# A fused QKV projection on one Trainium2 core: the K index renumbered, and the weights loaded one k-slice per transfer

## The chip, the cores and the metric

The kernel runs on one core of one Trainium2 chip, with one launch. The core has TensorE (PE, with its weight loads shown apart as PEld), VectorE (DVE), ScalarE (ACT), GpSimd (POOL) and SyncE (SP, which here only issues transfers), and sixteen DMA engines that move data between HBM and the on-chip SBUF. The metric is the device time of one execution in microseconds (us); lower is better.

## The reference

```python
batch, seq, hidden = 16, 512, 768
x: (16, 512, 768) float32,   w_qkv: (768, 2304) float32

qkv = np.matmul(x, w_qkv)
q = qkv[..., :hidden]; k = qkv[..., hidden:2*hidden]; v = qkv[..., 2*hidden:]
return np.stack([q, k, v], axis=0)          # (3, 16, 512, 768) float32
```

It is one product of 8192 rows by K = 768 by 2304 columns, whose three thirds of columns go to three places.

## The kernel before

**Tiling.** The 8192 rows of x are taken 256 at a time: 32 pairs of row tiles, p = 0 to 31. K = 768 is cut into KT = 6 slices of 128. The columns are cut into two "quads" of 1024 (q = 0 and 1, each two blocks of CB = 512, c = 0 and 1) and REM = 256 columns between them. PE contracts over the partition axis, so both operands must have k on the partitions. Which k lies on which partition is free, as long as x and w agree: before, partition p, slice j holds k = 6p + j.

**The weights.** `load_w` (L87) issues one transfer on SP for a range of slices of one column block. `load_blocks` (L93) calls it: for (q, c) = (0, 0) with one slice per transfer (six transfers of 256 KB), for the other three blocks with three slices per transfer (two of 768 KB each). The 256 remaining columns, tile `str`, come in one transfer with six slices. All of w is 7.08 MB, loaded once in the first part of the program. fp32 staging tiles `st` are then cast: into `b1` and `bt` (bf16, by DVE at L413 and L373, by ACT at L371), `b22` (L441, L456), `w_rem` (L426, L427), and differences t1 to t4 for the second method (`sum_w`, L113).

**The first three pairs (p = 0, 1, 2)** run plainly in bf16, in `block` (L375): the six row tiles times one 512-column block at a time, in the order (q, c) = (0,0), (0,1), (1,0), (1,1). Their x comes by `load_rows` (L138) with rows on the partitions; `cast_rows` (L153) makes bf16 (DVE L145 and L149, ACT L147), `turn_rows` (L160) has PE transpose 128x128 tiles (L167) and copies them out of PSUM. Eleven and then four matmuls on zeros (`busy`, L361) stand before real work.

**All later pairs (p = 3 to 31)** use Strassen's seven products with Winograd's sums (`do`, L220; matmuls L212), two in bf16 and five in fp32r, for both quads at once (`two`, L275), and `rem` (L260 to L273) for the other 256 columns. Their x comes by `load_x` (L122): four transfers per pair, each putting a quarter of the columns, 192, on 32 partitions. Then `transpose` (L128, instruction L130) turns 32x32 blocks on DVE, `round_x` (L173, instruction L175) casts to bf16 on POOL, and `sums_x` (L177) forms the sums on POOL.

**What sets the order.** The order is written out by hand; each engine and each issuing queue takes its instructions in the program's order. On SP: `load_rows(0)`, `load_rows(1)`, six transfers of block (0,0), `str`, `load_rows(2)`, then blocks (0,1), (1,0), (1,1), `load_x(3)`, the stores of remaining columns and of block results, with `load_x(4)` among them. On ACT, `block` puts the casts of the next block (`cast_next`, L409) ahead of the evictions of the even row tiles (L394) of p = 0 and 1. The pool `o` has five buffers; `str` and six quads of the first three pairs share them, so the fifth and sixth quads wait for stored ones. `bt0` and `bt1` share one buffer. PSUM has eight banks.

Of the kernel before, what the change touches and what calls it, by code (L numbers as in the profile page):

```python
# [10 lines left out]
def kernel(  # L11
# [20 lines left out]
    nc = tc.nc  # L32
    P = 128
    G = 32
    B, T, H = x.shape
    M = B * T
    K = H
    N3 = w_qkv.shape[1]
    KT = K // P
# [45 lines left out]


    def load_w(dst, j0, nj, off, cols):  # L87
        rows = w_qkv.rearrange("(p j) n -> p j n", j=KT)
        nc.sync.dma_start(dst, rows[:, j0:j0 + nj, off:off + cols])

    stage = {}

    def load_blocks(q, c, nj=KH):  # L93
        if q == 0:
            t = tq_pool.tile([P, KT, CB], fp32, name="st0", tag="tq")
            for j in range(0, KT, nj):
                load_w(t[:, j:j + nj], j, nj, Q_OFF[q] + c * CB, CB)
            stage[q, 0, c], stage[q, 1, c] = t[:, :KH, :], t[:, KH:, :]
        else:
            for h in range(2):  # L100
                t = st_pool.tile([P, KH, CB], fp32, name="st1", tag="st")
                load_w(t[:], h * KH, KH, Q_OFF[q] + c * CB, CB)
                stage[q, h, c] = t[:]
# [11 lines left out]
    xin, xf, xb, sr = {}, {}, {}, {}  # L115
# [12 lines left out]
    def transpose(p):  # L128
        t = xf_pool.tile([P, KT, 2 * P], fp32, name="xf")
        nc.vector.transpose(  # L130
            t[:].rearrange("p j (g b) -> p g j b", b=G),
            xin.pop(p)[:].rearrange("p g (a j) -> p g j a", a=G),
        )
        xf[p] = t

# [7 lines left out]
    def copy_halves(dst, src, two):  # L143

        nc.vector.tensor_copy(out=dst[0], in_=src[0])  # L145
        if two:
            nc.scalar.activation(dst[1], src[1], ident)  # L147
        else:
            nc.vector.tensor_copy(out=dst[1], in_=src[1])  # L149

    xc = {}

    def cast_rows(p, two=True):  # L153
        src = xin.pop(p)
        xc[p] = s_pool.tile([P, 2, K], bf16, name="xc", tag="s")
        for r in range(2):
            halves = (slice(0, K // 2), slice(K // 2, K))
            copy_halves([xc[p][:, r, n] for n in halves], [src[:, r, n] for n in halves], two)

    def turn_rows(p, two=True):  # L160
        c = xc.pop(p)
        xb[p] = xb_pool.tile([P, KT, 2 * P], bf16, name="xb", tag="xb")
        for r in range(2):
            cols = c[:, r, :].rearrange("m (p j) -> m j p", j=KT)
            ps = ps_pool.tile([P, KT, P], bf16, name="ps")
            for j in range(KT):
                nc.tensor.transpose(ps[:, j, :], cols[:, j, :], eye)  # L167
            ks = (slice(0, KH), slice(KH, KT))
            copy_halves(
                [xb[p][:, n, r * P:(r + 1) * P] for n in ks], [ps[:, n, :] for n in ks], two  # L170
            )
# [179 lines left out]
    load_blocks(0, 0, 1)  # L351
    st_rem = o_pool.tile([P, KT, REM], fp32, name="str", tag="o")
    load_w(st_rem[:], 0, KT, R_OFF, REM)
    load_rows(2)
    load_blocks(0, 1)
# [59 lines left out]
    nothing = lambda p: None  # L415
    busy(11)
    cast_rows(0)
    turn_rows(0)
    busy(4)
    cast_rows(1)  # L420
    cast_k(0)
    cast_k(1)
    turn_rows(1)
    for j in range(2, KT):
        cast_k(j)
# [6 lines left out]
    rem(0)  # L432
    rem(1)
    cast_rows(2, False)
    turn_rows(2, False)
    block(0, 0, b1[0], halves((4, 5)), nothing)
    for h in range(2):
# [11 lines left out]
    sum_w(1, 1)  # L449
    sum_w(1, 2)  # L450
    transpose(3)
    round_x(3)
    sums_x(3)
# [4 lines left out]
    for p in range(NS, NP):  # L458
        def early():
            if p + 1 < NP:  # L460
                transpose(p + 1)
                round_x(p + 1)
                sums_x(p + 1)
            if p + 2 < NP:
                load_x(p + 2, nc.scalar)

        if p < NP - 1:
            two(quad(p, 0), quad(p, 1), early)
        else:
            last(quad(p, 0), quad(p, 1))  # L470
# [30 lines left out]
```

## Time and profile before

| what | value |
|---|---|
| three timed runs | 362.67, 362.73, 363.09 us; median 362.73 |
| the profiled execution: span, first to last instruction | 361.3 us |
| around the span, against that median | 1.4 us |
| PE busy | 353.4 us, 98% of the span |
| DVE, ACT, POOL busy | 224.4, 182.9, 173.9 us |
| `STREAM_TRANSPOSE` L130 on DVE | 29 times, 2950 ns each |
| HBM read, written | 32.24 MB, 75.50 MB |

The profile's own total time is not listed apart from the three timed runs, so its span is set against their median. Busy time is the time in which an engine had an instruction in work. The chain that ended last is followed backwards from the final instruction to whatever released it; shares of that chain say where the time is set, while busy shares of engines off the chain say only how much room they have. A time at which a transfer lands is read from the first instruction that waited for it.

### The profile page before, as it was taken

The numbers are of one execution on the slowest core, as the hardware profiler recorded it, in microseconds if no ns is written. First come the engines' busy times: TensorE is split into PE (matmuls) and PEld (weight loads), VectorE is DVE, ScalarE is ACT, GpSimd is POOL, SyncE is SP. The second block draws the span as 40 slices with busy tenths as digits, with TensorE's granted clock in tenths as the row PEclk, the third lists the DMA queues.
The fourth block names the chain that finished last, engine by engine and source line by source line (L and its number), as shares of the span: only waits on it lengthen the run. The fifth ranks groups of instructions, "written<-read, shape, count | busy, mean of one in ns | idle before, by whom it ended". The sixth has DMA issues, their size and how long they took to land.

```text
span 361.3 us, 5221 instructions
## 1 busy us (share of the span) xinstructions
PE 353.4 (98%) x1765; PEld 251.0 (69%) x1797; DVE 224.4 (62%) x239; ACT 182.9 (51%) x304; POOL 173.9 (48%) x180
## 2 busy tenths in 40 slices
PE   8999999999999999999999999999999999999995
PEld 3644577777777777777777777777777777777763
DVE  3499826765566765566675565676556676556642
ACT  4547555455454545454545445455545454545452
POOL 0001861746664445664445665444665444666410
PEclk9999999999999999999999999999999999999999
DMA  7999869988898999899899999998989899999666
GB/s 298 405 388 373 286 221 359 331 289 295 278 328 301 294 273 294 276 324 315 280 280 290 281 308 309 291 289 278 292 288 321 295 300 271 297 272 339 264 261 232
DMA packets 80617, 108.08 MB, mean 299 GB/s; under 512 B 4816, under 2 KB 60368, under 8 KB 80592
## 3 DMA queue, kind: packets, MB, share of 16 engines
q1 hardware_dynamic: 65184, 96.35, 80.8%
q10 hardware_dynamic: 15408, 11.41, 9.6%
q8 instruction: 14, 0.23, 0.3%
q14 instruction: 11, 0.09, 0.1%
HBM read 32.24 MB, written 75.50 MB: 298 GB/s over the span
## 4 chain that ended last, share of the span: by engine, by line
PE 96%; ACT 1%; issue 1%; ACTq 0%; DVE 0%
PE ps L212 75%; PE ps L262 11%; PE ps L385 9%; PE ps L365 1%; PE ps L167 1%; ACT o L243 0%; ACTq L303 0%; ACT xb L147 0%; ACT orem L317 0%; DVE xb L145 0%; ACT xc L147 0%; ACTq L319 0%; DVE zero L346 0%; ACTq L317 0%
## 5 line engine op out<-in xcount | busy, mean ns | idle before, releaser
L212 PE MATMUL ps<-t,s 128*128 128x512 f32 x696 | 173.8, 398 | 0.0
L212 PEld LDWEIGHTS ps<-t,s 128*128 128x128 f32 x696 | 130.7, 188 | 29.7
L175 POOL CAST xb<-xf 128x1536 bf16<-128x1536 f32 x29 | 43.8, 1510 | 168.3 <-DVE xf L130 156.0
L240 DVE TENSOR_TENSOR o<-o,ps 128x512 f32<-128x512 f32 x58 | 39.9, 688 | 91.2 <-ACT o L239 91.2
L130 DVE STREAM_TRANSPOSE xf<-xin 128x1536 f32<-128x1536 f32 x29 | 85.5, 2950 | 3.7 <-DMA out_dram<-orem 2.1
L212 PE MATMUL ps<-b,xb 128*128 128x512 bf16 x320 | 82.4, 380 | 1.5
L239 ACT ACTIVATE o<-ps 128x512 f32<-128x512 f32 x58 | 34.8, 600 | 44.2 <-PE ps L212 44.2
L212 PEld LDWEIGHTS <-xb 128*128 128x128 bf16 x348 | 31.7, 98 | 35.6 <-issue 7.3
L233 ACT ACTIVATE o<-ps 128x512 f32<-128x512 f32 x58 | 34.9, 601 | 42.1 <-PE ps L212 39.4
L246 DVE TENSOR_TENSOR o<-o,ps 128x512 f32<-128x512 f32 x58 | 39.9, 688 | 21.3 <-PE ps L212 20.2
L212 PE MATMUL ps<-b,s 128*128 128x512 f32 x174 | 48.7, 389 | 0.0
L262 PE MATMUL ps<-w_rem,xb 128*128 128x256 bf16 x384 | 47.2, 273 | 0.0
L243 ACT ACTIVATE o<-ps 128x512 f32<-128x512 f32 x58 | 34.7, 599 | 24.1 <-PE ps L212 21.3
L226 ACT ACTIVATE o<-ps 128x512 f32<-128x512 f32 x58 | 34.7, 598 | 23.8 <-DVE o L246 20.6
L262 PEld LDWEIGHTS <-xb 128*128 128x128 bf16 x384 | 37.4, 98 | 11.2 <-issue 0.5
L230 DVE TENSOR_TENSOR o<-o,ps 128x512 f32<-128x512 f32 x58 | 36.5, 673 | 5.4 <-PE ps L212 4.1
L212 PEld LDWEIGHTS ps<-b,s 128*128 128x128 f32 x174 | 32.7, 188 | 6.8
L184 POOL TENSOR_TENSOR s<-s,xf 128x384 fp32r<-128x384 f32 x29 | 30.0, 1035 | 2.3
L183 POOL TENSOR_TENSOR s<-xf 128x384 fp32r<-128x384 f32 x29 | 30.9, 1064 | 0.0
L185 POOL TENSOR_TENSOR s<-xf 128x384 fp32r<-128x384 f32 x29 | 29.5, 1017 | 0.0
L187 POOL TENSOR_TENSOR s<-xf,s 128x384 fp32r<-128x384 f32 x29 | 29.5, 1016 | 0.0
L272 ACT ACTIVATE orem<-ps 128x512 f32<-128x512 f32 x31 | 18.5, 598 | 20.7 <-PE ps L262 19.5
(36 smaller groups left out, 129.4 us busy)
## 6 DMA issues: line engine op xcount, KB each, us to landing
out_dram<-o SPq DMA_DIRECT2D x62, 768.0 KB, 4.8
out_dram<-o SPq DMA_DIRECT2D x65, 256.0 KB, 4.1
xin<-in_x_dram SPq DMA_DIRECT2D x62, 192.0 KB, 6.9
xin<-in_x_dram ACTq DMA_DIRECT2D x54, 192.0 KB, 4.4
out_dram<-orem SPq DMA_DIRECT2D x31, 256.0 KB, 5.7
st<-in_w_qkv_dram SPq DMA_DIRECT2D x6, 768.0 KB, 13.1
xin<-in_x_dram SPq DMA_DIRECT2D x3, 768.0 KB, 5.7
st<-in_w_qkv_dram SPq DMA_DIRECT2D x6, 256.0 KB, 6.1
```

Of the source, the lines that this page charges most:

```text
L130: nc.vector.transpose(t[:].rearrange("p j (g b) -> p g j b", b=G), xin.pop(p)[:].rearrange("p g (a j) -> p g j a", a=G),)
L175: nc.gpsimd.tensor_copy(out=xb[p][:], in_=xf[p][:])
L212: nc.tensor.matmul(ps[:], lhs[j], rhs[j], start=(start and j == 0), stop=(j == KH - 1), skip_group_check=True,)
L226: nc.scalar.activation(c11, u.x[:], ident)
L230: nc.vector.tensor_tensor(c11, c11, u.z[:], op=add)
L233: nc.scalar.activation(c12, u.x[:], ident)
L239: nc.scalar.activation(c22, u.x[:], ident)
L240: nc.vector.tensor_tensor(c22, c22, u.y[:], op=add)
L243: nc.scalar.activation(c21, u.x[:], ident)
L246: nc.vector.tensor_tensor(c12, c12, u.y[:], op=add)
L262: nc.tensor.matmul(ps, xb[p][:, j, r * P:(r + 1) * P], w_rem[j // KH][:, j % KH, :], start=(j == 0), stop=(j == KT - 1), skip_group_check= ...
L385: nc.tensor.matmul(ps[n][:], xb[p][:, j, r * P:(r + 1) * P], w[:, j, :], start=(j == 0), stop=(j == KT - 1), skip_group_check=True,)
```

## The change

The K index is numbered anew: k = 192 i + 32 j + a, with i in 0..3, j in 0..5, a in 0..31. Partition 32 i + a, slice j holds that k. So:

- `load_w` sees w as four bands of 192 rows; slice j takes 32 neighbouring rows from each band. It issues one transfer per slice where it issued one for a range of slices: `str` becomes six transfers of 128 KB, and the blocks (0,1), (1,0) and (1,1) become six of 256 KB each where they were two of 768 KB. Block (0,0) had six transfers and keeps six, with the new rows.
- `transpose` reads, for each 32x32 block, 32 neighbouring fp32 elements of a partition where it read every sixth one.
- `cast_rows` writes its bf16 columns in the order (j, i, a), while it reads them in the order of k; each half is two of the four bands.
- `turn_rows` then takes 128 neighbouring columns for slice j where it took every sixth one.

```diff
     def load_w(dst, j0, nj, off, cols):
-        rows = w_qkv.rearrange("(p j) n -> p j n", j=KT)
-        nc.sync.dma_start(dst, rows[:, j0:j0 + nj, off:off + cols])
+        rows = w_qkv.rearrange("(i j a) n -> i a j n", i=4, a=G)
+        for j in range(nj):
+            nc.sync.dma_start(dst[:, j], rows[:, :, j0 + j, off:off + cols])
...
         nc.vector.transpose(
             t[:].rearrange("p j (g b) -> p g j b", b=G),
-            xin.pop(p)[:].rearrange("p g (a j) -> p g j a", a=G),
+            xin.pop(p)[:].rearrange("p g (j a) -> p g j a", a=G),
         )
...
         for r in range(2):
-            halves = (slice(0, K // 2), slice(K // 2, K))
-            copy_halves([xc[p][:, r, n] for n in halves], [src[:, r, n] for n in halves], two)
+            turned = xc[p][:, r].rearrange("m (j i a) -> m i j a", i=4, a=G)
+            rows = src[:, r].rearrange("m (i j a) -> m i j a", i=4, a=G)
+            halves = (slice(0, 2), slice(2, 4))
+            copy_halves([turned[:, n] for n in halves], [rows[:, n] for n in halves], two)
...
-            cols = c[:, r, :].rearrange("m (p j) -> m j p", j=KT)
+            cols = c[:, r, :].rearrange("m (j p) -> m j p", j=KT)
```

## The prediction

> **What bounds the kernel now.** I read the page's chain first, to see which engine sets the end; then the chain in order of time, to see whether any stretch differs; then the timeline where the first three pairs end; then the busy time by stretches of the start, where all of w is loaded.
>
> The page, parts 1 and 4 (shares of the span), and three rows of part 6 (issues, KB each, median us to landing):
>
> ```profile
> PE 353.4 (98%) x1765; PEld 251.0 (69%) x1797; DVE 224.4 (62%) x239; ACT 182.9 (51%) x304; POOL 173.9 (48%) x180
> ...
> PE 96%; ACT 1%; issue 1%; ACTq 0%; DVE 0%
> ...
> st<-in_w_qkv_dram SPq DMA_DIRECT2D x6, 768.0 KB, 13.1
> xin<-in_x_dram SPq DMA_DIRECT2D x3, 768.0 KB, 5.7
> st<-in_w_qkv_dram SPq DMA_DIRECT2D x6, 256.0 KB, 6.1
> ```
>
> PE sets 96% of the chain, so DVE's 224 us count for nothing unless something late on DVE reaches PE. In order of time the chain runs through PE without a gap of more than 0.1 us from 18.5 us to the end of the last pair. The timeline (start, us, engine, line) at the end of the first three pairs:
>
> ```profile
> 28.42 7.93 PE L385 MATMUL ps<-b,xb 128*128 128x512 bf16 x35
> ...
> 34.29 1.48 ACT L371 ACTIVATE bt<-st 128x1536 bf16<-128x1536 f32 x1
> ...
> 36.19 7.93 PE L385 MATMUL ps<-bt,xb 128*128 128x512 bf16 x35
> ...
> 43.96 1.47 PE L262 MATMUL ps<-w_rem,xb 128*128 128x256 bf16 x12
> ...
> 45.27 1.46 PE L212 MATMUL ps<-b,xb 128*128 128x512 bf16 x6
> ```
>
> The reader sees two things: the last piece of w that PE needs is cast at 34.29, by ACT, which waited for no transfer there (the page of waits has 0.4 us for `st` in all); and Strassen pair p = 3 begins at 45.4. From there each pair takes 10.74 us of PE. Last, the start by stretches (busy us of each engine, granted clock, DMA share, GB/s):
>
> ```profile
> 2.40:5.00 2.60, 2.60 (x7) 0.91 (x6) 0.09 (x1) 0.09 (x1) 0.00 (x0) 1.00 0.97 376
> ...
> 10.00:15.00 5.00, 4.95 (x26) 2.48 (x26) 2.00 (x6) 2.20 (x4) 0.00 (x0) 1.00 1.06 403
> 15.00:20.00 5.00, 4.83 (x41) 3.46 (x41) 3.38 (x10) 2.19 (x5) 0.00 (x0) 1.00 1.05 406
> 20.00:25.00 5.00, 5.00 (x25) 2.29 (x24) 4.97 (x4) 2.68 (x3) 0.00 (x0) 1.00 1.05 406
> ...
> 240.00:280.00 40.00, 39.79 (x201) 29.82 (x203) 24.87 (x26) 20.16 (x35) 22.89 (x24) 1.00 0.93 300
> ```
>
> From 2.4 us the sixteen DMA engines are full at 403 to 406 GB/s until w is in: 25.3 GB/s for each engine. The start is thus a race of the loads against PE, and PE wins it by little.
>
> **The change part by part.**
>
> *The DVE transposes.* 29 of 2950 ns. The nearest row that reads neighbouring fp32 elements of the same size, the 128x1536 differences of L113, takes 1751 ns; at that, 29 x 1.2 = 35 us of DVE work go. Bounds: 0 and 35 us off DVE. On the time I put nothing, since PE waits for no transpose after p = 3; POOL waits 156 us in all for L130, but POOL itself has 187 us to spare. If DVE's room were gone, the cost would be the wait of L175. PE's 10.74 us per pair remain.
>
> *The casts of the first rows.* Four DVE and four ACT casts for p = 0, 1 (354 and 516 ns) and four on DVE for p = 2. Written in runs of 32 they may slow on DVE. From 384 to 1536 elements a DVE cast goes from 354 to 953 ns, 0.52 ns an element and 154 ns of start; L113's row gives (1751 - 154)/1536 = 1.04 ns an element. At that rate a cast takes 553 ns, so four lose 0.8 us: bounds 0 and 0.8. PE's reads of `xc` gain neighbouring columns: weight loads L167 take 132 ns against 98 ns on `xb`, 24 on the chain, 0 to 0.8 us saved. I take zero for both: what follows hides them, since PE will wait for w.
>
> *Loading w.* This is the step that decides. The number of packets, their size (2 KB, 1 KB for `str`) and the bytes stay. What moves is the number of issues on SP, 13 to 30, and the shape. An issue costs SP 0.4 to 0.5 us where the ring is not full, so 17 more are about 8 us of SP; by bytes the w transfers alone keep SP waiting, so this is hidden if the transfers still run at full width. But the shape changes: until now both sides of every transfer begin with a count that sixteen divides (128 or 768 rows of w, 32 or 128 of x). Now the HBM side begins with four bands whose distance, 192 rows, cannot be folded with the 32 rows inside; the SBUF side begins with 128. No row of before shows how such a transfer is dealt out. The ends are sixteen engines (405 GB/s, nothing lost) and one engine for each band, four (4 x 25.3 = 101 GB/s). I take four: the only cut that falls on the leading step of both sides is that into the four bands, and every full-width row has a leading count that sixteen divides, so none speaks for sixteen here.
>
> [...]
>
> *What four engines make of the start.* Each of those four carries, in SP's order, in KB of 1024: x rows 0 and 1, 96; block (0,0), 6 x 64 = 384; `str`, 6 x 32 = 192; x rows 2, 48; then 384 for each of (0,1), (1,0), (1,1). Together 1872 KB = 1.917 MB, at 25.3 GB/s 75.8 us. Data begins at 2.4; the first x rows (0.786 MB at 405 GB/s, done by 4.3) were used at 4.92, so 0.6 us from bytes to use. The last half block is usable at 2.4 + 75.8 + 0.6 = 78.8 us.
>
> Its cast on ACT (L371) started at 34.29 and now starts at 78.8: 44.5 us later. Against that, PE has run ahead with the first half of block (1,1), whose data come 7.8 us earlier. It gets as far as four of the six row tiles, because the evictions that free further banks stand behind that cast on ACT: 12 matmuls of 0.216 us, 2.6 us gained. For some 5 us before that cast PE has nothing to do. The first eleven matmuls of the trace, after idleness, took 4.88 us, against 11 x 0.216 = 2.38: 2.5 us lost to a slow start. The bounds are 0 and 2.5; I take 2.0, near the only start that the trace has, less a little because the first six wait for banks anyway. (The stretches print a granted clock of 1.00 there too, so the column will not show it.)
>
> [...]
>
> Queued behind the loads on SP are `load_x(3)`, two stores of remaining columns, three quads' stores (64 KB per engine each, 2.6 us), `load_x(4)`. On the four late engines `load_x(3)` lands near 81; then L130, L175 (2.8 us the first time) bring xb to 84 to 86, against p = 3's start at 89. The first quad's store lands near 85, and the eviction of the sixth quad waits for its buffer: 0 to 3 us, inside the same wait, so nothing added, 3 kept for the upper end. From p = 3 on nothing differs, and there the DMA engines, at 0.93 share, take the backlog of stores within a pair or two.
>
> Sum: 44.5 - 2.6 + 2.0 = 43.9 us. Span 361.3 + 43.9 = 405.2; with the 1.4 us between this span and the median of the runs, 406.6.
>
> **The rivals.**
>
> *Sixteen engines, and a gain (faster).* Place: PE's transposes of the first rows, which stand on the chain. Price: up to 0.8 us, 361.9. It decides only if the transfers keep full width, and if PE then finds the first slices of b1 in place (cast at 7.96, first used at 9.3: 0.5 us to spare). Against it: the leading count of four.
>
> *Sixteen engines, nothing to see.* The gain is eaten by slower casts, and `str` in six issues (6 x 0.45 for 0.65 us) pushes `load_rows(2)` by up to 1 us, about the slack that its casts have (done at 16.0, PE free at 17.0). 362.7, within 0.2%; a little more push gives 363.5. For it: packets are unchanged and SP is held back by full rings anyway.
>
> *Eight engines.* 144 + 6912/8 = 1008 KB per engine, 40.8 us, usable at 43.8: 9.5 us late, 372 us. I see no cut into eight in either pattern.
>
> *Four engines at another rate* is a bound, not a rival: if an engine alone is faster than its sixteenth (shares over 1.00 say that packets overlap; I allow 7%), 5 us less, and without the slow start 2 less: 399. Slower: the steady stretch moves 300 GB/s at 0.93, 20.2 GB/s per engine, which would give 425; but it holds 768-byte packets, w does not, so I go half way: 416, with the buffer wait 418.
>
> **How the numbers follow.** Four engines 0.86; eight 0.03; sixteen with a loss over 0.2% 0.03, unchanged 0.06, gain 0.02. So slower 0.92, same 0.06, faster 0.02, where 0.2% (0.7 us) is about what a measurement can tell from no change. Range 398 to 418, holding most of the first case, some 0.82; prediction 406.6.
>
> **What would show it.** In the profile after: DMA at about a quarter of its share and near 100 GB/s from some 6 to 75 us; ACT's and DVE's casts of `st` waiting for transfers of w; PE busy in under half of that stretch; L371's last cast near 79; p = 3 near 89; L130 shorter, near 1.75 us, with DVE's total down by some 35 us and pairs still 10.74 us apart. Wrong if DMA runs at 400 GB/s through 25 us: then the bands do not narrow the transfer, and the time stays within 1 us of before.

## The result, and the profile after

The changed kernel takes 410.28 us (median of four runs, 410.12 to 411.08) against 362.70 us before (362.50 to 363.09): 1.132 times as long, 95% interval 1.130 to 1.133. The profiled execution took 410.42 us, with a span of 408.6. (One of the ten executions of the second experiment below ran at a lower granted clock, 0.85, took 406.21 us and is left out of its median.)

The page of the changed kernel, busy time (part 1), PE's busy tenths, granted clock, DMA share and GB/s in 40 slices of 10.2 us (part 2), the chain by engine and line (part 4), and the issues of the staging tiles (part 6, without a time to landing here). Lines of the code stand three further down than before: L90 issues w, L131 is the DVE transpose, L374 ACT's casts of w, L388 the matmuls of the first three pairs, L215 those of the later ones.

```profile
PE 369.1 (90%) x1765; PEld 254.5 (62%) x1797; DVE 194.9 (48%) x239; ACT 182.0 (45%) x304; POOL 173.6 (42%) x180
...
PE   7548576579999999999999999999999999999995
...
PEclk9856966969999999999999999999999999999999
DMA  5252222798999889999998999999999899999956
GB/s 192 102 148 104 102 102 102 222 340 276 366 374 323 294 292 292 294 286 289 287 291 298 293 293 286 288 288 305 308 297 305 290 296 290 293 296 297 309 211 255
...
PE 77%; SPq 15%; DMA 4%; issue 1%; ACT 1%; ACTq 0%
PE ps L215 66%; SPq L90 15%; PE ps L265 9%; DMA st<-in_w_qkv_dram 4%; PE ps L388 2%; SPq L142 1%; ACT o L246 0%; ACTq L306 0%; ACT orem L320 0%; ACT o L397 0%; ACTq L322 0%; ACTq L320 0%; ACT bt L374 0%
...
st<-in_w_qkv_dram SPq DMA_DIRECT2D x24, 256.0 KB
```

Nearly a fifth of the chain, which was PE from end to end, now belongs to w: SP stands in L90, where an issue takes 2.44 us in the median (ns, min/median/max, in the view of the tile `st`), about the 2.57 us in which 256 KB move at 102 GB/s, and then the last transfer lands:

```profile
L90 SPq DMA_DIRECT2D st<-in_w_qkv_dram x24: 537/2442/4392, 1.7 to 65.5; - x24
```

The damage lies in the first nine slices; from the tenth on PE reads 9 in every slice but the last, as before. The same in stretches (busy us by engine, granted clock, DMA share, GB/s):

```profile
2.40:5.00 2.60, 2.60 (x7) 0.91 (x6) 0.01 (x1) 0.01 (x1) 0.00 (x0) 1.00 0.95 373
...
10.00:20.00 10.00, 5.27 (x15) 1.86 (x16) 1.96 (x7) 0.87 (x2) 0.00 (x0) 0.83 0.26 102
...
40.00:50.00 10.00, 4.96 (x23) 1.97 (x21) 2.17 (x3) 1.19 (x2) 0.00 (x0) 1.00 0.26 102
...
80.00:90.00 10.00, 6.16 (x18) 2.44 (x19) 7.87 (x4) 4.71 (x8) 4.17 (x2) 0.66 1.00 370
...
240.00:280.00 40.00, 39.79 (x200) 29.18 (x203) 22.78 (x28) 19.75 (x34) 20.49 (x21) 1.00 0.93 292
```

The first row is x, at full width (share 0.95, 373 GB/s). Then w flows at 102 GB/s, and the DMA share of 0.26 says how much of the engines that takes: as much as four of sixteen, each as busy as before (1.05 x 4/16 = 0.26). The share is a mean over the engines, and no view lists them one by one; that few of them work, and not all of them a little, is the author's reading, and the probe of the leading count below fits it. (A packet of 2 KB took 84 ns in the median in both traces.) The timeline at the end of the first three pairs (start, us, engine, line):

```profile
64.16 1.48 ACT L374 ACTIVATE b<-st 128x1536 bf16<-128x1536 f32 x1 [5.25 <-DMA st<-in_w_qkv_dram]
...
71.85 1.48 ACT L374 ACTIVATE bt<-st 128x1536 bf16<-128x1536 f32 x1 [4.26 <-DMA st<-in_w_qkv_dram]
...
73.92 2.75 PE L388 MATMUL ps<-bt,xb 128*128 128x512 bf16 x12
...
81.60 1.48 ACT L374 ACTIVATE bt<-st 128x1536 bf16<-128x1536 f32 x1 [7.29 <-DMA st<-in_w_qkv_dram]
...
91.17 1.47 PE L265 MATMUL ps<-w_rem,xb 128*128 128x256 bf16 x12
92.48 1.46 PE L215 MATMUL ps<-b,xb 128*128 128x512 bf16 x6
```

The last cast of w starts at 81.60 (34.29 before), after 7.29 us of waiting for its transfer, and p = 3 begins at 92.65 by the chain (45.43 before). The two pieces of the chains, first the kernel before, then the changed one:

```profile
45.43 1.30 PE ps L212 x6
```

```profile
92.65 1.29 PE ps L215 x6
```

From there to the end of the span it is 315.95 us, before 315.87: nothing in the steady part has changed, although DVE's 29 transposes fell from 2950 to 1772 ns each.

### The profile page after: what moved, and what is told of

It reads as the page before. It is cut to its first block, busy times and chain, and to the rows that moved or that the text cites. A ratio compares the mean times of both kernels' runs of the same rounds, so it can differ in the third digit from the quotient of the medians.

```text
span 408.6 us, 5248 instructions
## 1 busy us (share of the span) xinstructions
PE 369.1 (90%) x1765; PEld 254.5 (62%) x1797; DVE 194.9 (48%) x239; ACT 182.0 (45%) x304; POOL 173.6 (42%) x180
## 4 chain that ended last, share of the span: by engine, by line
PE 77%; SPq 15%; DMA 4%; issue 1%; ACT 1%; ACTq 0%
PE ps L215 66%; SPq L90 15%; PE ps L265 9%; DMA st<-in_w_qkv_dram 4%; PE ps L388 2%; SPq L142 1%; ACT o L246 0%; ACTq L306 0%; ACT orem L320 0%; ACT o L397 0%; ACTq L322 0%; ACTq L320 0%; ACT bt L374 0%
## 5 line engine op out<-in xcount | busy, mean ns | idle before, releaser
L215 PE MATMUL ps<-t,s 128*128 128x512 f32 x696 | 173.8, 398 | 0.0
L215 PEld LDWEIGHTS ps<-t,s 128*128 128x128 f32 x696 | 130.8, 188 | 29.7
L215 PE MATMUL ps<-b,xb 128*128 128x512 bf16 x320 | 82.6, 380 | 1.5
L243 DVE TENSOR_TENSOR o<-o,ps 128x512 f32<-128x512 f32 x58 | 39.9, 688 | 90.5 <-ACT o L242 90.5
L131 DVE STREAM_TRANSPOSE xf<-xin 128x1536 f32<-128x1536 f32 x29 | 51.4, 1772 | 9.4 <-DMA xin<-in_x_dram 5.2
L265 PE MATMUL ps<-w_rem,xb 128*128 128x256 bf16 x384 | 49.9, 282 | 6.6 <-ACT w_rem L429 4.2
L215 PEld LDWEIGHTS <-xb 128*128 128x128 bf16 x348 | 31.7, 98 | 35.6 <-issue 7.3
L233 DVE TENSOR_TENSOR o<-o,ps 128x512 f32<-128x512 f32 x58 | 38.6, 686 | 25.9 <-ACT orem L275 22.8
L265 PEld LDWEIGHTS <-xb 128*128 128x128 bf16 x384 | 38.4, 101 | 19.9 <-issue 5.0
L249 DVE TENSOR_TENSOR o<-o,ps 128x512 f32<-128x512 f32 x58 | 39.9, 688 | 21.5 <-PE ps L215 20.4
L215 PE MATMUL ps<-b,s 128*128 128x512 f32 x174 | 48.8, 390 | 0.0
L388 PEld LDWEIGHTS <-xb 128*128 128x128 bf16 x144 | 16.5, 116 | 51.5 <-issue 40.0
L215 PEld LDWEIGHTS ps<-b,s 128*128 128x128 f32 x174 | 32.6, 188 | 7.0 <-POOL xb L178 0.3
L388 PE MATMUL ps<-b,xb 128*128 128x512 bf16 x69 | 23.7, 495 | 13.2 <-DVE b L416 6.3
L388 PE MATMUL ps<-bt,xb 128*128 128x512 bf16 x71 | 20.0, 444 | 12.2 <-ACT o L397 7.0
L186 POOL TENSOR_TENSOR s<-xf 128x384 fp32r<-128x384 f32 x29 | 30.9, 1067 | 0.0
```

Of the source, the lines that this page charges most:

```text
L131: nc.vector.transpose(t[:].rearrange("p j (g b) -> p g j b", b=G), xin.pop(p)[:].rearrange("p g (j a) -> p g j a", a=G),)
L215: nc.tensor.matmul(ps[:], lhs[j], rhs[j], start=(start and j == 0), stop=(j == KH - 1), skip_group_check=True,)
L233: nc.vector.tensor_tensor(c11, c11, u.z[:], op=add)
L243: nc.vector.tensor_tensor(c22, c22, u.y[:], op=add)
L249: nc.vector.tensor_tensor(c12, c12, u.y[:], op=add)
L265: nc.tensor.matmul(ps, xb[p][:, j, r * P:(r + 1) * P], w_rem[j // KH][:, j % KH, :], start=(j == 0), stop=(j == KT - 1), skip_group_check= ...
```

## The experiments

Theory A is the prediction's: a transfer whose HBM side begins with four bands goes to four engines. Its rivals: B, the many issues on SP are what is slow; C, the new rows are slow to read.

**One transfer for each band.**

```diff
         rows = w_qkv.rearrange("(i j a) n -> i a j n", i=4, a=G)
-        for j in range(nj):
-            nc.sync.dma_start(dst[:, j], rows[:, :, j0 + j, off:off + cols])
+        for i in range(4):
+            nc.sync.dma_start(dst[i * G:(i + 1) * G], rows[i, :, j0:j0 + nj, off:off + cols])
```

> The changed kernel with one edit: load_w issues one transfer per band i (32 rows of partitions, all its slices) where it issued one per slice (four bands). The numbering of K, the DVE transposes and the casts stay as changed; both sides of every w transfer now begin with 32. SP issues 52 transfers of w where the changed kernel has 30 and the kernel before 13. Theory A (a transfer is dealt to as many engines as its leading count allows, four for four bands): DMA is back at 400 GB/s from 2.4 us, the last cast of w (L374) starts near 34 us, the time is that of the kernel before, 362 to 364 us. Theory B (the number of issues on SP, 2.4 us each in the changed kernel, makes the loads slow): with 52 issues later still, the time over 410 us. Theory C (the new order of rows in HBM is slow to read, whoever reads it): the same rows are read, so about 410 us.

Measured: 375.24 us (373.95 to 375.46), 1.033 of before (1.032 to 1.035). More issues and 35 us less, so B falls, and C cannot hold most of the loss. But A's 362 to 364 was missed by 11 us. Stretches of this run:

```profile
10.00:15.00 5.00, 3.05 (x13) 1.14 (x12) 1.23 (x4) 0.67 (x2) 0.00 (x0) 1.00 0.53 141
...
30.00:35.00 5.00, 5.00 (x25) 2.25 (x23) 4.17 (x3) 1.80 (x3) 0.00 (x0) 1.00 1.06 243
```

Two things are new. Up to 15 us SP's issues are the limit: transfers of 64 KB at 0.46 us each (0.42 and the step to the next) give 141 GB/s with the engines half idle. Later all sixteen are busy (1.06), and still only 243 GB/s flow: from 30 to 35 us a 2 KB packet takes 144 ns in the median, not 84.

**The kernel before, with one transfer per slice.**

```diff
         rows = w_qkv.rearrange("(p j) n -> p j n", j=KT)
-        nc.sync.dma_start(dst, rows[:, j0:j0 + nj, off:off + cols])
+        for j in range(nj):
+            nc.sync.dma_start(dst[:, j], rows[:, j0 + j, off:off + cols])
```

> The kernel before with one edit: one transfer per slice everywhere, 30 issues of w on SP as in the changed kernel, each beginning with 128 on both sides, old numbering. Theory A: at full width, 362 to 364 us; str in six issues may push load_rows(2) by up to 1 us, which its casts' slack just takes. Theory B: the loads become as late as in the changed kernel, 405 to 412 us. Theory C: 362 to 364 us.

Measured: 362.80 us, ratio 1.000 (0.999 to 1.001). Thirty issues that begin with 128 cost nothing, `str` in six pieces included. B is settled.

**The leading count by itself.**

```diff
+    for lead in (128, 16, 8, 4, 2):
+        ...     # rows: "(p j) n -> p j n" for 128, else "(i j a) n -> i a j n" with i=lead
+        for j in range(3):
+            nc.sync.dma_start(t[:, j * CB:(j + 1) * CB], src)      # 256 KB each
+        for j in range(3):
+            nc.vector.tensor_copy(out=tiny[:], in_=t[:, j * CB:j * CB + 1])
```

> The kernel before with a probe behind its end: five groups, each of three transfers of 256 KB of w into one scratch tile, waited for by DVE before the next group. The HBM side begins with 128, 16, 8, 4 and 2 in turn, the SBUF side always with 128. Theory A, at 25.4 GB/s for an engine: 786 KB take 1.9, 1.9, 3.9, 7.7 and 15.5 us, each plus some 2 to 3 us of issue and landing; DMA rates of 405, 405, 203, 102 and 51 GB/s inside the groups; about 45 us added in all, 405 to 412 us. Theories B and C: all five groups take the same 2 us plus 2 to 3, about 25 us added.

Measured: 398.71 us, 36 more than before (about 45 expected). The timeline of the probe: DVE's copy that waited for the second and the third transfer of each group, for leads of 128, 16, 8, 4, 2:

```profile
361.45 0.15 DVE L483 COPY tiny<-xf 128x1 f32<-128x1 f32 x1 [0.55 <-DMA xf<-in_w_qkv_dram]
362.06 0.15 DVE L483 COPY tiny<-xf 128x1 f32<-128x1 f32 x1 [0.46 <-DMA xf<-in_w_qkv_dram]
...
365.35 0.15 DVE L483 COPY tiny<-xf 128x1 f32<-128x1 f32 x1 [0.79 <-DMA xf<-in_w_qkv_dram]
366.33 0.15 DVE L483 COPY tiny<-xf 128x1 f32<-128x1 f32 x1 [0.83 <-DMA xf<-in_w_qkv_dram]
...
370.13 0.15 DVE L483 COPY tiny<-xf 128x1 f32<-128x1 f32 x1 [1.20 <-DMA xf<-in_w_qkv_dram]
371.47 0.15 DVE L483 COPY tiny<-xf 128x1 f32<-128x1 f32 x1 [1.18 <-DMA xf<-in_w_qkv_dram]
...
377.51 0.15 DVE L483 COPY tiny<-xf 128x1 f32<-128x1 f32 x1 [2.40 <-DMA xf<-in_w_qkv_dram]
380.06 0.15 DVE L483 COPY tiny<-xf 128x1 f32<-128x1 f32 x1 [2.40 <-DMA xf<-in_w_qkv_dram]
...
390.33 0.15 DVE L483 COPY tiny<-xf 128x1 f32<-128x1 f32 x1 [4.99 <-DMA xf<-in_w_qkv_dram]
395.44 0.15 DVE L483 COPY tiny<-xf 128x1 f32<-128x1 f32 x1 [4.96 <-DMA xf<-in_w_qkv_dram]
```

Between the second and third of a group lie 0.61, 0.98, 1.34, 2.55 and 5.11 us. For 262 KB that is 196, 103 and 51 GB/s at leads of 8, 4 and 2, with DMA shares of 0.50, 0.26 and 0.13 inside the groups: what eight, four and two engines would carry at 25 GB/s each (405 over sixteen). The same SBUF side, the same bytes, the same queue; what differs is the leading count and with it how many rows of w stand side by side, and neighbouring rows cost nothing visible in a later probe (4.76 us for 128 of them). So in this probe the rate goes with the leading count from 8 down. Lead 16 at 0.98 looked slower than 128.

**Leads from 16 to 128 again.**

```diff
-    for lead in (128, 16, 8, 4, 2):
+    for lead in (16, 32, 64, 128, 16):
```

> The probe behind the kernel before again, now with HBM sides that begin with 16, 32, 64, 128 and once more 16 (three transfers of 256 KB each, the SBUF side always 128 partitions). In the first probe three transfers of lead 16 came 0.97 us apart (270 GB/s) where sixteen full engines would need 0.65. Theory H (any HBM side of more than one leading count is dealt out in a slower way): 16, 32 and 64 stay near 0.97 us apart, only 128 at 0.65. Theory I (the wider the lead, the better the rows are spread): 32 between them, 64 at 0.65 to 0.75. Whichever holds, lead 16 twice shows whether place in the series matters.

Measured: 380.22 us. The first and the last copy of the groups 128 and 16 (the second time):

```profile
371.22 0.15 DVE L483 COPY tiny<-xf 128x1 f32<-128x1 f32 x1 [1.32 <-DMA xf<-in_w_qkv_dram]
...
373.01 0.15 DVE L483 COPY tiny<-xf 128x1 f32<-128x1 f32 x1 [0.48 <-DMA xf<-in_w_qkv_dram]
...
374.75 0.15 DVE L483 COPY tiny<-xf 128x1 f32<-128x1 f32 x1 [1.59 <-DMA xf<-in_w_qkv_dram]
...
376.95 0.15 DVE L483 COPY tiny<-xf 128x1 f32<-128x1 f32 x1 [0.54 <-DMA xf<-in_w_qkv_dram]
```

From first to last it is 1.96, 2.12, 2.13, 1.79 and 2.20 us for 16, 32, 64, 128 and 16. Lead 16 differs from itself by 0.24, and one gap of lead 16 is now 0.70. Neither H nor I: three transfers are too few to tell wide leads apart, and the 0.98 was no property of lead 16.

**The rest of the change alone.** The changed kernel with the old `load_w` (and so another matrix product, as the expectation says).

```diff
-        rows = w_qkv.rearrange("(i j a) n -> i a j n", i=4, a=G)
-        for j in range(nj):
-            nc.sync.dma_start(dst[:, j], rows[:, :, j0 + j, off:off + cols])
+        rows = w_qkv.rearrange("(p j) n -> p j n", j=KT)
+        nc.sync.dma_start(dst, rows[:, j0:j0 + nj, off:off + cols])
```

> The changed kernel with the load_w of the kernel before: 13 transfers of w that begin with 128, so w at full width. Its rows of w are in the old order while x is in the new one, so it computes another matrix product of the same size and cost; everything else is the change (DVE transposes of neighbours, casts in runs of 32, PE's transposes of neighbouring columns). It tells what the rest of the change is worth. Prediction as on record: L131 takes 1771 ns as in the changed kernel, nothing of it reaches the time: 362.3 to 363.2 us, pairs of 10.74 us. Rival (the shorter transposes give POOL or PE room somewhere, up to 0.35 us a pair): 352 to 361 us. Rival (slower casts of the first rows): 363.5.

Measured: 362.56 us, ratio 1.000 (0.999 to 1.001). Its page, part 1, and the transpose's row in the view of the tile `xf` (min/median/max ns):

```profile
PE 355.0 (98%) x1797; PEld 250.7 (69%) x1797; DVE 194.6 (54%) x239; ACT 182.5 (51%) x304; POOL 173.7 (48%) x180
```

```profile
L130 DVE STREAM_TRANSPOSE xf<-xin x29: 1770/1771/1778, 31.5 to 335.9; 128x1536 f32<-128x1536 f32 x29
```

DVE is 30 us less busy than before, and the time is the same. The whole loss of the change, 47.6 us, is thus the loading of w.

**`load_x(3)` ahead of the last block.** A smaller question: the casts of the last three half blocks stand 7.69 and then 9.75 us apart in the changed kernel, where 786 KB at 102 GB/s take 7.7.

```diff
     load_blocks(1, 0)
+    load_x(3, nc.sync)
     load_blocks(1, 1)
-    load_x(3, nc.sync)
```

> The changed kernel with load_x(3) issued ahead of block (1,1) of w. For the 2 us by which the last half block of w came later than 7.7 us after the half before it (9.75 us). Theory D (what is queued behind w takes turns with it on the four engines): only the stores of remaining columns stand behind w now, so the two last casts (L374) are 7.7 to 9.0 us apart, the last one at 81 to 82.5 us, and the time is 409 to 411 us. Theory E (strict order on each engine, the last piece is late for another reason): both halves move by the 2 us that load_x(3) takes, the casts stay 9.7 us apart, the last one near 83.5 us, and the time is near 412 us.

Measured, in one run: 411.96 us. The timeline's casts in this run:

```profile
56.35 1.48 ACT L374 ACTIVATE b<-st 128x1536 bf16<-128x1536 f32 x1 [16.04 <-DMA st<-in_w_qkv_dram]
...
66.07 1.48 ACT L374 ACTIVATE b<-st 128x1536 bf16<-128x1536 f32 x1 [7.26 <-DMA st<-in_w_qkv_dram]
...
75.91 1.48 ACT L374 ACTIVATE bt<-st 128x1536 bf16<-128x1536 f32 x1 [6.41 <-DMA st<-in_w_qkv_dram]
...
83.56 1.48 ACT L374 ACTIVATE bt<-st 128x1536 bf16<-128x1536 f32 x1 [5.20 <-DMA st<-in_w_qkv_dram]
```

The gaps are 9.72, 9.84 and 7.65: D's gap at the end, E's time. The piece that stands in the queue in front of `load_x(3)` (block (1,0), second half) comes 2 us later than it did, and the piece behind it comes 2 us later again. So the load of x does delay the four-band transfer in front of it, and it costs its own time too. The sizes of the packets in this trace show that not everything that moves beside w does so. From 64 to 68 us, where x moves (packets of 768 bytes), w's packets of 2 KB carry 61 and then 33 GB/s. From 74 to 82 us stores (packets of 1 and 3 KB) move 64 to 301 GB/s beside w, and w keeps its 102. How the load gets at the transfer in front was not tried.

**Work for PE in the last wait.** 32 matmuls of zeros, added to an unfinished sum.

```diff
                 if KT - 1 not in js:
+                    if n == 3:
+                        for _ in range(warm):          # 32 in block (1, 1), else 0
+                            nc.tensor.matmul(ps[n][:], zero[:, :P], zero[:],
+                                             start=False, stop=False, skip_group_check=True)
                     continue
```

> The changed kernel with 32 matmuls of zeros added to an unfinished sum, just before PE's last wait for w (block (1,1), behind the first half of its first four row tiles): 7 us of PE work in a wait of 7 us, and the result is the same. Its price is the slow start after the wait, which the prediction put at 2.0 us (0 to 2.5). If right: the matmuls after the wait stand 0.216 us apart where they stand 0.43, and the time is 407.8 to 408.6 us. If PE's evictions on ACT set the pace there: 409.5 to 410.4 us.

Measured: 409.60 us (409.10 to 409.91), 0.7 less than the changed kernel, whose range is 410.12 to 411.08. The timeline here (in this kernel L395 are the zeros):

```profile
76.81 7.07 PE L395 MATMUL ps<-zero 128*128 128x512 bf16 x32
...
83.71 5.34 PE L388 MATMUL ps<-bt,xb 128*128 128x512 bf16 x24
88.89 1.47 PE L265 MATMUL ps<-w_rem,xb 128*128 128x256 bf16 x12
90.20 1.46 PE L215 MATMUL ps<-b,xb 128*128 128x512 bf16 x6
```

The 24 matmuls stand 0.216 us apart, and p = 3 begins at 90.37 where it began at 92.65: the slow start cost 2.3 us. Of these 0.7 reach the time, which so lies in the range given for the other case, though the matmuls after the wait stand as close as the first case said. One wait took part of the place: in pair 4 PE waits until 110.18 for DVE, whose transpose L131 waited for the x of the next pair until 106.49; from pair 5 on this run is 1.75 us ahead, not 2.3. A further microsecond goes at the end of the profiled run, where one store's issue on ACT (L322) takes 1.46 us instead of 0.37; why was not tried.

**Why one band at a time is slow.** A probe and three runs on the 243 GB/s of the first experiment; none of them beats the kernel before.

```diff
+    # behind the kernel before, 786 KB a group, to t[:, 0:3, 0:512]:
+    # old rows to 128 partitions; neighbouring rows to 128; old rows in four transfers to 32;
+    # the bands' rows in four to 32; old rows in two to 64
```

> Why transfers of one band (32 partitions) ran at 245 GB/s with all sixteen engines at work, in the kernel with one transfer per band (375.2 us). The kernel before with a probe behind its end: five groups of 786 KB each, waited for one after the other: one transfer to 128 partitions with the old rows of w; the same with 128 neighbouring rows; four transfers to 32 partitions with the old rows; four with the rows of the bands; two to 64 partitions with the old rows. Theory F (SBUF side: few partitions are written at a time): the 128s take 1.9 us of transfer at 405 GB/s, both kinds of 32 take 3.2 us at 245 GB/s, 64 between them or at 405. Theory G (HBM side: neighbouring rows are slow to read): the second and fourth group are at 245 GB/s, the others at 405.

Measured: 388.04 us. From group to group 4.76 us (128, neighbouring rows), 5.84 (32, old rows), 5.58 (32, the bands' rows) and 6.06 (64); the first group overlaps the kernel's last stores. The kind of rows makes no difference beyond 0.3 us, so theory G (and C) has nothing for it; but a group is too short to separate the rate from the issues, and F is not shown by it.

```diff
         for i in range(4):
-            nc.sync.dma_start(dst[i * G:(i + 1) * G], rows[i, :, j0:j0 + nj, off:off + cols])
+            (nc.sync, nc.gpsimd)[i % 2].dma_start(
+                dst[i * G:(i + 1) * G], rows[i, :, j0:j0 + nj, off:off + cols])
```

> The kernel with one transfer per band, the bands 0 and 2 issued on SP and 1 and 3 on POOL, so that two bands are in flight at a time. Theory F: 64 partitions are written at once, 330 to 405 GB/s, and SP has half of the issues: 364 to 369 us. Theory G, or a limit that counts packets: stays at 245 GB/s, 372 to 376 us.

Measured: 369.98 us (369.30 to 370.70), between the two ranges. The issue limit at the start is gone (253 GB/s from 10 to 15 us, 141 with SP alone), the low rate later is not:

```profile
25.00:30.00 5.00, 4.13 (x20) 1.68 (x18) 1.40 (x2) 1.20 (x2) 0.00 (x0) 1.00 1.05 259
30.00:35.00 5.00, 4.62 (x21) 1.95 (x20) 4.97 (x4) 0.99 (x1) 0.00 (x0) 1.00 1.04 245
```

```diff
-            (nc.sync, nc.gpsimd)[i % 2].dma_start(
+            (nc.sync, nc.gpsimd)[i // 2].dma_start(
```

> The kernel with one transfer per band on two queues, dealt out differently: bands 0 and 1 on SP, 2 and 3 on POOL, so that band 0 is in flight beside band 2, and 1 beside 3, where the run before had 0 beside 1. [...] Theory Q (transfers to 32 partitions are slow whatever is beside them, or POOL's issues set the rate): 250 to 280 GB/s, 369 to 371 us.

Measured: 369.23 us (368.75 to 369.70).

```diff
-        for i in range(4):
+        for i in (0, 2, 1, 3):
             nc.sync.dma_start(dst[i * G:(i + 1) * G], rows[i, :, j0:j0 + nj, off:off + cols])
```

> The kernel with one transfer per band, all on SP, in the order 0, 2, 1, 3 where it was 0, 1, 2, 3. [...] Theory Q: 245 GB/s and 374 to 375.5 us.

Measured: 374.03 us (373.99 to 374.58). Stretches of the two last runs, first the order 0, 2, 1, 3 on one queue (243 GB/s in the order 0, 1, 2, 3):

```profile
30.00:35.00 5.00, 5.00 (x25) 2.27 (x24) 4.30 (x3) 2.68 (x3) 0.00 (x0) 1.00 1.01 290
```

then bands 0 and 1 on SP beside 2 and 3 on POOL:

```profile
25.00:30.00 5.00, 5.00 (x23) 2.19 (x22) 2.56 (x3) 1.19 (x2) 0.00 (x0) 0.96 1.05 311
30.00:35.00 5.00, 5.00 (x25) 2.26 (x24) 4.96 (x4) 2.67 (x4) 0.00 (x0) 1.00 1.07 208
```

From 20 to 30 us, while both queues carry w, keeping bands of one half of the partitions apart gives 312 and 311 GB/s where the run with 0 beside 1 had 256 and 259, a fifth more. From 10 to 20 us it gives nothing (260 and 273 against 253 and 281), and from 10 to 35 us it nowhere exceeds 312 GB/s, where the kernel before has 403 to 406 until w is in. From 30 to 35 us POOL's transfers are done, and SP moves bands 0 and 1 alone, both of partitions 0 to 63: 208 GB/s, about half of 405, with 164 ns for a 2 KB packet. That is the lowest rate of the four runs with all engines busy. The times are those of theory Q (369 to 371, and 374 to 375.5).

So the runs show that it matters which bands are in flight together (208 GB/s for bands 0 and 1 alone, 311 and 312 with 2 and 3 beside them); that two bands which lie apart move at 330 GB/s or more, as I had expected, they do not show. What holds such a pair at 311 stays open.

## Why the prediction was right

The forecast was 406.6 us, slower, 398 to 418; the measured time is 410.3. The course is the one named: a transfer cut into four bands moved at a quarter of the full rate, w came late, and PE waited for its last piece. That a transfer of four bands goes to four engines was the author's choice between two ends, which no row of before decides; what the runs show for it is the share of 0.26 with 102 GB/s, and the probe's shares of 0.50, 0.26 and 0.13 at leads of 8, 4 and 2.

| step of the prediction | predicted | measured |
|---|---|---|
| engines for a transfer of w | 4 of 16, 101 GB/s | DMA share 0.26, 102 GB/s |
| last cast of w starts | 78.8, 44.5 later | 81.60, 47.3 later |
| from that cast to p = 3, against before | 12 matmuls ahead (-2.6), slow start (+2.0): -0.6 | 12 matmuls ahead, slow start 2.3; 11.05 us against 11.14: -0.1 |
| from p = 3 to the end of the span | 0 | +0.1 |
| around the span | 1.4 us | 1.8 us (410.42 - 408.6) |
| L130/L131 | near 1751 ns, no gain in time | 1772 ns, no gain (362.56 alone) |

**The mis-sized term** is the last landing, 2.8 us of the 3.8 by which the profiled run (410.42) missed 406.6; the rest is 0.5, 0.1 and 0.4 in the three rows below it. The sum took the four engines' share of every transfer in turn. It held to 0.1 us up to the end of block (0,0) (22.4 predicted, cast at 22.54), lost 1.2 us at `str` (30.2 predicted, cast at 31.39), of which 0.9 remain at block (1,0), and 2.0 us at the last half block. Both losses stand where a load of x follows in the queue, `load_rows(2)` and `load_x(3)`. The run with `load_x(3)` moved shows for that load that it delays the piece in front; for `load_rows(2)` this is only likely. The 0.4 around the span was an error of pairing: the 1.4 sets the span of one run against the median of three, while an execution of the kernel before with a span of 361.3 us is on record at 363.11, 1.8 more, as after.

**The slow start** was sized well (2.0 against 2.3) but one remark on it was wrong: the granted clock does show it, at 0.50 from 82 to 88 us, though the first eleven matmuls of the trace stand under 1.00:

```profile
80.00:81.00 1.00, 0.00 (x0) 0.00 (x0) 0.00 (x0) 0.00 (x0) 0.00 (x0) 1.00 1.07 417
81.00:82.00 1.00, 0.00 (x0) 0.00 (x0) 0.34 (x1) 0.40 (x1) 0.00 (x0) 0.82 1.04 406
82.00:83.00 1.00, 0.00 (x0) 0.00 (x0) 1.00 (x1) 1.00 (x2) 0.00 (x0) 0.50 0.73 254
```

The matmuls had stopped at 76.67, and a mean of 0.82 from 81 to 82, between 1.00 and 0.50, puts the fall at 81.6, 5.0 us later; in the wait before it the matmuls stopped at 62.29, and 0.64 from 64 to 66 puts it at 64.6, 2.3 us later. Both times are estimates from these means, and the two falls did not come equally long after the last matmul.

One sign was missed: PE was to be busy in under half of the stretch from 6 to 75 us and was busy in 43.6 of its 69 us, at a mean granted clock of 0.75, so that its matmuls took longer.

**What was costed at nothing** was right: the transposes (362.56 with everything but the loads), the casts (DVE 356 and ACT 523 ns against 354 and 516), the issues on SP (362.80 with thirty; no view shows a ring, only issues of w that take SP 0.37 to 1.81 us in the kernel before), and the wait of the sixth quad's eviction for its buffer (no L397 waits for a store). PE's weight loads from `xc` did fall, from 125 to 98 ns in the median, and nothing of it reaches the time. **The rivals** with sixteen and with eight engines fall with the DMA share of 0.26 and with the probe, where leads of 8 and 4 ran at 196 and 103 GB/s.

## What to carry to other kernels

Before a load is reshaped, write down the count that each side begins with once the strides are folded: here a renumbering of rows turned 128 into 4 by 32, and with it 405 GB/s into 102, without changing a byte or a packet. The DMA share in the profile says it at once (0.26 where it was 1.05), while SP's long issues only look like the cause. And a faster engine that is not on the chain, here 30 us off DVE, buys nothing: price the parts of a change apart, since the harmless-looking line was the dear one.

## What the runs showed of the hardware that was not expected

- A full DMA share is not yet the full rate. At a share of 1.06, transfers to one band of 32 partitions after the other moved 243 GB/s, and a 2 KB packet took 144 ns in the median instead of 84. Bands 0 and 1 alone, the lower half of the partitions, moved 208 GB/s; with bands of the other half in flight beside them it was 311 and 312; on one queue from 20 to 35 us the order 0, 2, 1, 3 gave 271 to 290 and the order 0, 1, 2, 3 gave 243 to 265.
- A load of x queued behind a four-band transfer of w delayed the one in front by 2 us (gaps of 9.75 and 9.72 us against 7.7); stores beside it did not (7.65).
- Removing 2.3 us from PE's path gave 0.7 us back in time.
